# Layer 0's feed-forward: input projection by seven products of quarters

## The chip, the cores and the metric

One core of a Trainium2 chip. The metric is the time of one execution in device microseconds, median of the runs; lower is better.

## The reference

The kernel computes two transformer layers on one latent sequence of 256 tokens and one context of 256 tokens, with model width 1024. What the change touches is the gated feed-forward of layer 0, which both sequences pass (512 tokens together):

```python
def swiglu(h, w_in, w_out):
    a, u = jnp.split(h @ w_in, 2, axis=-1)
    return (jax.nn.silu(a) * u) @ w_out
...
D_FF = -(-(8 * D_MODEL) // (3 * 256)) * 256      # 2816
...
x_lat = x_lat + g2 * swiglu(rms_norm(x_lat, norm2_g[i]) * (1 + sc2) + sh2, ffn_w_in[i], ffn_w_out[i])
x_ctx = x_ctx + cg2 * swiglu(rms_norm(x_ctx, norm2_g[i]) * (1 + csc2) + csh2, ffn_w_in[i], ffn_w_out[i])
```

`w_in` is 1024 x 5632 (gate and up side by side), `w_out` is 2816 x 1024, all float32.

## The kernel before

Everything lies with features on the 128 partitions and tokens along the free axis: eight tiles of 128 features by 512 tokens, latent tokens in columns 0 to 255 (`LAT`), context tokens in 256 to 511 (`CTX`).

Every float32 product is made of three. A value is split into a high part (a copy to the `fp32r` type, on ScalarE, L402) and a low part (the value less its high part, on VectorE, L403). `prod` (L410) adds high x high, high x low and low x high into one PSUM bank. The activations' parts are `hh[k]` and `hl[k]`, made by `modulate` (L363 to L367) after each norm. A block of weights is loaded by a DMA on SyncE's queue into `w_raw` (two buffers), and split by `weights` into `w_hi` and `w_lo` (two buffers each).

`ffn(0, ...)` walks the inner width of 2816 (22 tiles of 128) in two chunks of 12 and 10 tiles. In a chunk, for each pair of tiles, it loads a gate block and an up block (1024 rows by 256 columns each), makes four banks of 512 tokens by 24 products each, and from them Silu(gate) x up, split again into `mid_h` and `mid_l` (L692 to L697). The first pair is made in two halves of 256 tokens, since the context's activations come later. Then four groups of 256 output columns (`mc`) multiply the chunk's mids by `w_out`, and VectorE adds the result, times a gate, onto the residual `x` (L446). After the last chunk the next norm's sums are taken from `x` (`after`).

Beside that run the ada steps (`ada_aside`): six parameter vectors of modulation, eight steps each. A step loads 128 rows of `ada_w` and multiplies and adds them onto one or two accumulators of 1024 columns on VectorE (L317, L319), two for the first three parameters (24 steps), one for the last three. `next(steps)` in the loops says where a step is written; here three per pair and two per `mc`.

The Tile framework orders each engine's instructions when the kernel is built, by priority and data dependence, and places all the semaphores. On the chip each engine runs its queue in that order. PSUM has eight banks of 512 float32 columns: `mixed()` hands out seven in turn, one is for ada.

GpSimd has next to no work in this stage. In the earlier attention layer it scales a bias table (L538) and masks it with two selects per half (L541, L545).

Of the kernel before, what the change touches and what calls it, by code (L numbers as in the profile page):

```python
# [8 lines left out]
F32 = mybir.dt.float32  # L9
F32R = mybir.dt.float32r  # L10
I32 = mybir.dt.int32
U8 = mybir.dt.uint8
AF = mybir.ActivationFunctionType
ALU = mybir.AluOpType
AX = mybir.AxisListType

P = 128
T = 512
D = 1024
KT = D // P  # L20
DFF = 2816
# [7 lines left out]
LAT = slice(0, 256)  # L29
CTX = slice(256, 512)  # L30
HALVES = ((0, LAT), (1, CTX))

NA_ADA = ((2,), (4,), (), (3,))
FFN_ADA = ((0, 5), (1, 1), (1, 0), (1, 2), (1, 4), (1, 3))


def cap(ap, off, dims):

    return bass.AP(ap.tensor, ap.offset + off, [list(ap.ap[0])] + [list(d) for d in dims])


class Block:
# [701 lines left out]
        ctx.close()  # L744


    def hgrn(self):
        nc = self.nc
        self.masks()
        yctx, ctx = ExitStack(), ExitStack()  # L750
# [6 lines left out]
        wi = self.in_hg_w_in[0]  # L757
        for hp in range(4):
            def wblock(i):
                return self.weights(wi[:, i * D + hp * 256 : i * D + (hp + 1) * 256])  # L760

            f = [[None, None], [None, None]]
            for d in range(2):
                w = wblock(3 + d)
                banks = [self.mm() for _ in range(2)]
# [8 lines left out]
            def project(i):  # L774
                w = wblock(i)
                if i == 1:
                    v = gp.tile([P, 4, 256], F32, name="hv", tag="hv")
                    for b in range(2):
                        ps = self.mm()
                        for j in range(2):  # L780
                            self.toks(ps[:, j * 256 : (j + 1) * 256], w, 2 * b + j)
                        nc.scalar.copy(v[:, 2 * b : 2 * b + 2].rearrange("p i c -> p (i c)"), ps)
                    return v
                ps = self.mm()
                for m in range(2):
                    self.feat(ps[:, m * 256 : (m + 1) * 256], w, m, LAT)
                t = gp.tile([P, T], F32, name=f"qg{i}", tag=f"qg{i}")
                nc.scalar.activation(t, ps, AF.Sigmoid)
                nc.vector.tensor_tensor(t, t, ps, op=ALU.mult)
                return t  # L790

            q = project(0)
# [6 lines left out]
            for m in range(2):  # L799
                h, on = 2 * hp + m, outs[m]  # L800
# [11 lines left out]
        wo = self.in_hg_w_o[0]  # L812
        self.norm_begin()
        for mc in range(4):
# [3 lines left out]
            else:  # L818
                own = lp if mc == 3 else None
                wh, wl = [[t[:, k] for k in range(KT)] for t in self.weights(block, pool=own)]  # L820
            one = self.mm()
            banks = [one[:, 0:256], one[:, 256:512] if mc < 3 else self.mm()[:, 0:256]]
# [178 lines left out]
    def finish(self, ctx):  # L1001
        nc = self.nc
        op = self.pool(ctx, "outp", 2)
        self.osb = [op.tile([P, 2, T], F32, name="osb", tag="osb") for _ in range(2)]

        def after(mt, s, c):
            half, q = mt // 4, mt % 4
            tp = self.mixed()
            for i in range(2):
                nc.tensor.transpose(tp[:, i * P : (i + 1) * P], self.x[mt][:, i * P : (i + 1) * P], self.ident)  # L1010
            nc.scalar.copy(
                self.osb[half][:, :, q * P : (q + 1) * P], tp[:, 0:256].rearrange("p (i c) -> p i c", i=2)
            )

            q0 = {3: 0, 5: 0, 6: 2, 7: 3}.get(mt)
            if q0 is not None:
                nc.sync.dma_start(
                    self.out[0, :, half * T + q0 * P : (mt + 1) * P].rearrange("(i p) c -> p i c", i=2),
                    self.osb[half][:, :, q0 * P : (q + 1) * P],
                )  # L1020

        return after

    def run(self):
        nc = self.nc
        self.setup()
        self.na_and_ada()

    def na_and_ada(self):
        self.na()  # L1030
        def after(mt, s, c):
            if mt == 0 and s == 0:
                self.norm_begin()
            self.norm_add(mt, c)
            if mt == KT - 1:
                self.norm_end(1, 0, s, c)

        self.ffn(0, slice(0, T), (12, 10), 14, after, lambda pool: self.ada_aside(FFN_ADA, pool))
        self.hgrn()
        with ExitStack() as ctx:  # L1040
            self.ffn(1, LAT, (NFF,), NFF, self.finish(ctx))
# [39 lines left out]
```

## Time and profile before

| what | value |
|---|---|
| runs | median 1169.7 us of 3 (1169.43 to 1171.44) |
| the profiled execution | 1168.13 us, its span 1166.3 us |
| TensorE busy | 1138.9 us, 98% of the span |
| VectorE busy | 778.7 us, 67% |
| ScalarE busy | 501.7 us, 43% |
| GpSimd busy | 74.5 us, 6% |

PE is TensorE, PEld its weight loads, DVE VectorE, ACT ScalarE, POOL GpSimd, SP SyncE. Matmuls are pipelined: one starts before the one in front has ended, so the time that a matmul costs is the distance between starts, not its duration. The same holds, by less, for neighbouring instructions on VectorE. In rows, a name such as `w_lo<-w_raw,w_hi` is output and inputs, `mm` and `ax` are PSUM banks, "L403" is the kernel's line, and "xN" says how many instructions a row holds.

### The profile page before, as it was taken

The numbers are of one execution on the slowest core, as the hardware profiler recorded it, in microseconds if no ns is written. First come the engines' busy times: TensorE is split into PE (matmuls) and PEld (weight loads), VectorE is DVE, ScalarE is ACT, GpSimd is POOL, SyncE is SP. The second block draws the span as 40 slices with busy tenths as digits, with TensorE's granted clock in tenths as the row PEclk, the third lists the DMA queues.
The fourth block names the chain that finished last, engine by engine and source line by source line (L and its number), as shares of the span: only waits on it lengthen the run. The fifth ranks groups of instructions, "written<-read, shape, count | busy, mean of one in ns | idle before, by whom it ended". The sixth has DMA issues, their size and how long they took to land.

```text
span 1166.3 us, 21342 instructions
## 1 busy us (share of the span) xinstructions
PE 1138.9 (98%) x8539; PEld 987.2 (85%) x8539; DVE 778.7 (67%) x1872; ACT 501.7 (43%) x1079; POOL 74.5 (6%) x121
## 2 busy tenths in 40 slices
PE   6979989999999999999999999999999999999998
PEld 5968869887898787878887889889797988999998
DVE  4579776966697664845353778686768687556553
ACT  5356564745462232213223344434243465545442
POOL 1045331410000000000000000000000000000000
PEclk9999999999999999999999999999999999999999
DMA  9785452433337442636352651323232345564562
GB/s 330 252 211 94 118 131 73 64 130 124 107 93 229 135 170 94 230 136 216 130 194 68 199 167 46 100 74 110 73 110 74 99 175 197 182 210 158 197 217 87
DMA packets 134403, 169.23 MB, mean 145 GB/s; under 512 B 4609, under 2 KB 122273, under 8 KB 134305
## 3 DMA queue, kind: packets, MB, share of 16 engines
q1 hardware_dynamic: 132368, 164.64, 42.5%
q0 software_dynamic: 1728, 3.17, 3.2%
q8 instruction: 67, 1.10, 0.4%
q14 instruction: 32, 0.25, 0.1%
q10 hardware_dynamic: 208, 0.07, 0.0%
HBM read 166.82 MB, written 1.05 MB: 144 GB/s over the span
## 4 chain that ended last, share of the span: by engine, by line
PE 90%; DVE 4%; DMA 3%; ACT 2%; issue 1%; ACTq 0%; DVEq 0%
PE mm L410 49%; PE ax L410 28%; DMA ada_raw<-in_ada_w_dram 3%; PE ada_ps L216 2%; PE ax L651 2%; PE ax L902 1%; PE ax L613 1%; PE ax L579 1%; PE ax L637 1%; PE ax L885 1%; PE ax L580 1%; PE ada_ps L266 1%; ACT qs L569 1%; DVE w_lo L403 1%; PE ax L948 1%; PE ax L659 1%
## 5 line engine op out<-in xcount | busy, mean ns | idle before, releaser
L403 DVE TENSOR_TENSOR w_lo<-w_raw,w_hi 128x512 fp32r<-128x512 f32 (+1 forms) x448 | 272.5, 644 | 128.4 <-ACT w_hi L402 126.0
L402 ACT CAST w_hi<-w_raw 128x512 fp32r<-128x512 f32 (+1 forms) x448 | 238.0, 583 | 230.6 <-PE mm L410 100.3
L410 PE MATMUL mm<-hl,w_hi 128*128 128x256 f32 (+1 forms) x608 | 201.6, 333 | 0.0
L410 PE MATMUL mm<-hh,w_lo 128*128 128x256 f32 (+1 forms) x608 | 201.3, 332 | 0.0
L410 PE MATMUL mm<-hh,w_hi 128*128 128x256 f32 (+1 forms) x608 | 199.1, 329 | 0.0
L410 PE MATMUL ax<-hh,w_lo 128*128 128x256 f32 (+1 forms) x400 | 131.7, 330 | 0.0
L410 PE MATMUL ax<-hh,w_hi 128*128 128x256 f32 (+1 forms) x400 | 131.7, 329 | 0.0
L410 PE MATMUL ax<-hl,w_hi 128*128 128x256 f32 (+1 forms) x400 | 131.3, 328 | 0.0
L410 PE MATMUL mm<-w_hi,hh 128*128 128x256 f32 x448 | 126.3, 282 | 0.8 <-ACT hh L366 0.8
L410 PE MATMUL mm<-w_lo,hh 128*128 128x256 f32 x448 | 125.7, 280 | 0.0
L410 PE MATMUL mm<-w_hi,hl 128*128 128x256 f32 x448 | 125.5, 280 | 0.0
L410 PEld LDWEIGHTS mm<-hl,w_hi 128*128 128x128 f32 x608 | 114.1, 188 | 11.4
L410 PEld LDWEIGHTS mm<-hh,w_lo 128*128 128x128 f32 x608 | 114.0, 188 | 11.3
L410 PEld LDWEIGHTS mm<-hh,w_hi 128*128 128x128 f32 x608 | 113.8, 188 | 10.9 <-ACT hh L366 0.8
L319 DVE SCALAR_TENSOR_TENSOR ada_acc<-ada_raw,cs,ada_acc 128x1024 f32<-128x1024 f32 x63 | 79.0, 1280 | 19.4 <-DMA ada_raw<-in_ada_w_dram 19.2
L410 PEld LDWEIGHTS mm<-w_hi,hh 128*128 128x128 f32 x448 | 84.6, 189 | 5.1 <-issue 3.2
L410 PEld LDWEIGHTS mm<-w_hi,hl 128*128 128x128 f32 x448 | 84.2, 188 | 2.0 <-issue 1.6
L410 PEld LDWEIGHTS mm<-w_lo,hh 128*128 128x128 f32 x448 | 84.2, 188 | 1.8 <-issue 1.4
L410 PEld LDWEIGHTS ax<-hh,w_hi 128*128 128x128 f32 x400 | 75.2, 188 | 7.6 <-ACT w_hi L402 0.8
L410 PEld LDWEIGHTS ax<-hl,w_hi 128*128 128x128 f32 x400 | 75.1, 188 | 7.4
L410 PEld LDWEIGHTS ax<-hh,w_lo 128*128 128x128 f32 x400 | 74.9, 187 | 7.4 <-DVE w_lo L403 0.2
L696 ACT CAST mid_h<-sa 128x512 fp32r<-128x512 f32 (+1 forms) x44 | 22.5, 512 | 92.8 <-DVE sa L693 92.8
(278 smaller groups left out, 2133.3 us busy)
## 6 DMA issues: line engine op xcount, KB each, us to landing
w_raw<-in_ffn_w_in_dram SPq DMA_DIRECT2D x44, 1024.0 KB, 5.1
ada_raw<-in_ada_w_dram SPq DMA_DIRECT2D x80, 512.0 KB, 4.6
w_raw<-in_hg_w_in_dram SPq DMA_DIRECT2D x20, 1024.0 KB, 4.8
w_raw<-in_na_w_qkv_dram SPq DMA_DIRECT2D x9, 1024.0 KB, 5.0
ada_first<-in_ada_w_dram SPq DMA_DIRECT2D x32, 256.0 KB, 5.9
w_raw<-in_ffn_w_out_dram SPq DMA_DIRECT2D x8, 896.0 KB, 4.5
w_raw<-in_ffn_w_out_dram SPq DMA_DIRECT2D x8, 768.0 KB, 4.3
w_raw<-in_ffn_w_out_dram SPq DMA_DIRECT2D x8, 640.0 KB, 4.3
```

Source lines behind the costliest of these rows:

```text
L216: nc.tensor.matmul(ps[32 * j : 32 * j + 32, 0:256], cs[:, k, :], w[:, j * 256 : (j + 1) * 256], start=(k == 0), stop=(k == last), tile_pos ...
L266: nc.tensor.matmul(ps[32 * j : 32 * j + 32, 0:P], self.cs[:, k, :], w[:, j // 2, (j % 2) * P : (j % 2 + 1) * P], start=(k == 0), stop=(k = ...
L319: eng.scalar_tensor_tensor(acc[s], w, c, acc[s], op0=ALU.mult, op1=ALU.add)
L402: self.nc.scalar.copy(wh[:, ks], raw[:, ks])
L403: self.nc.vector.tensor_tensor(wl[:, ks], raw[:, ks], wh.bitcast(F32)[:, ks], op=ALU.subtract)
L410: self.nc.tensor.matmul(out, a, b, start=(start and i == 0 and j == 0), stop=(stop and i == n - 1 and j == 2), skip_group_check=True,)
L569: nc.scalar.activation(cap(qa[half], P - 1, back), src, AF.Copy, scale=self.q_gain[own])
L579: nc.tensor.matmul(ps, qs[a][:, t], ks[a][:, kr], start=True, stop=False, skip_group_check=True)
L580: nc.tensor.matmul(ps, self.ql[a][:, t], ks[a][:, kr], start=False, stop=True, skip_group_check=True)
L613: nc.tensor.transpose(tp[:, kt * P : (kt + 1) * P], sb[:, kt * P : (kt + 1) * P], self.ident)
L651: nc.tensor.matmul(o[64 * a : 64 * a + 64, 0:256], v[:, kt, j * P + 64 * a : j * P + 64 * a + 64], pts[a][0][:, kt], start=(kt == 0), stop ...
L696: nc.scalar.copy(mh, sa)
```

## The change

The input projection of layer 0 goes to a new function, `ffn_seven`, which replaces `ffn(0, ...)`; the inner width is cut into chunks of 8, 8 and 6 tiles instead of 12 and 10. The first pair of tiles is still made plainly (`plain`). For every other block of 1024 x 256 weights, a `unit` cuts the weights into four quarters of 512 x 128 and the activations into four of 512 features x 256 tokens, and makes the block's product from seven products of quarters instead of eight (Strassen's method in Winograd's form). The sums of activations (`s1`, `s2`, `s3`, `s4`) are made once (`sums`); `s3` overwrites the context half of the activations. The differences of weights (`t13`, `t2`, `t4`) are made for each unit on GpSimd. Each product is four tiles deep, three products each, 256 columns wide: 12 matmuls, 84 in a unit. The two PSUM halves `x` and `z` of one bank and a part `y` of another collect them, and copies and adds on ScalarE and VectorE join them to the two output tiles.

The weights' parts lie in a ring of eight places of 4 x 128 columns (`quarter`) which units and output projection fill in turn. Units interlace: a unit's last two products are written between the products of the next. The matmuls' order within a chunk is fixed by `add_manual_dep`. The low parts of the mids, and half of the low parts of the output weights, move from VectorE to GpSimd. The ada steps are spread anew: three after the plain pair, then one per unit, one per two units, one per unit in the three chunks, and two to four per `mc`.

```diff
+    def quarter(self, src, eng=None):
+        nc, n = self.nc, src.shape[1]
+        s = self.place % 8
+        self.place += 1
+        hi, lo = [...]
+        nc.scalar.copy(hi, src)
+        (eng or nc.vector).tensor_tensor(lo, src, hi.bitcast(F32), op=ALU.subtract)
+        return hi, lo
+
+    def ffn_seven(self, chunks, after, aside):
...
+        def finish(g, mh, ml):
+            nc.scalar.copy(mh, g)
+            nc.gpsimd.tensor_tensor(ml, g, mh.bitcast(F32), op=ALU.subtract)
+
+        def plain():
+            quarters = []
+            raws = [w_in(0, up) for up in range(2)]
...
+            banks = [self.mixed() for _ in range(4)]
+            for s, r in HALVES:
+                for bank, q in zip(banks, quarters):
+                    self.prod(bank[:, r], ...)
+                for k in range(KT):
+                    (nc.gpsimd if s == 0 else nc.vector).tensor_tensor(
+                        f[s][k // 2][:, k % 2], self.hh[k].bitcast(F32)[:, r], self.hl[k].bitcast(F32)[:, r], op=ALU.add
+                    )
+            sums()
...
+        def sums():
+            a, c = f
+            for p in range(2):
+                for out, x, y, op in (
+                    (c[2 + p], c[p], c[2 + p], ALU.add),
+                    (c[p], a[p], c[p], ALU.subtract),
+                    (a[p], c[2 + p], a[p], ALU.subtract),
+                    (a[2 + p], a[2 + p], a[p], ALU.subtract),
+                ):
+                    nc.vector.tensor_tensor(out, x, y, op=op)
+            for p in range(2):
+                for src, (hi, lo), k in ((c[2 + p], s1s, 0), (a[p], s24, 0), (a[2 + p], s24, 4)):
+                    ks = slice(k + 2 * p, k + 2 * p + 2)
+                    nc.scalar.copy(hi[:, ks], src)
+                    nc.vector.tensor_tensor(lo[:, ks], src, hi.bitcast(F32)[:, ks], op=ALU.subtract)
+            for k in range(4):
+                src, hi, lo = c[k // 2][:, k % 2], self.hh[k], self.hl[k]
+                nc.scalar.copy(hi[:, CTX], src)
+                nc.vector.tensor_tensor(lo[:, CTX], src, hi.bitcast(F32)[:, CTX], op=ALU.subtract)
...
+        def unit(raw, up, g, mids):
...
+            xz, y = self.mixed(), self.mixed()[:, 0:256]
+            x, z = xz[:, 0:256], xz[:, 256:512]
...
+            t13 = fp.tile([P, 2, 4, P], F32, name="t13", tag="t13", bufs=1)
+            t2 = fp.tile([P, 4, P], F32, name="t2", tag="t2", bufs=1)
+            t4 = fp.tile([P, 4, P], F32, name="t4", tag="t4", bufs=1)
+            run(x, self.quarter(b11), a11, True)
+            nc.scalar.copy(u[0][:, LAT], x)
+            run(y, self.quarter(b21), a12, True)
+            nc.vector.tensor_tensor(u[0][:, LAT], u[0][:, LAT], y, op=ALU.add)
+            yield
+            nc.gpsimd.tensor_tensor(t13, ..., op=ALU.subtract)
+            nc.gpsimd.tensor_tensor(t2, b22, t13[:, 0], op=ALU.subtract)
+            run(z, self.quarter(t13[:, 0]), s1)
+            nc.scalar.copy(u[1][:, CTX], z)
+            run(x, self.quarter(t2), s2)
+            nc.scalar.copy(u[1][:, LAT], x)
+            yield
+            nc.gpsimd.tensor_tensor(t4, b21, t2, op=ALU.subtract)
+            run(z, self.quarter(b22), s4)
+            nc.vector.tensor_tensor(u[1][:, LAT], u[1][:, LAT], z, op=ALU.add)
+            yield
+            run(x, self.quarter(t13[:, 1]), s3)
+            nc.vector.tensor_tensor(u[1][:, CTX], x, u[1][:, CTX], op=ALU.add)
+            if up:
+                nc.vector.tensor_tensor(g[0][:, LAT], g[0][:, LAT], u[0][:, LAT], op=ALU.mult)
+                nc.vector.tensor_tensor(g[1], g[1], u[1], op=ALU.mult)
+                finish(g[1], *mids[1])
+            else:
+                nc.scalar.activation(g[0][:, LAT], g[0][:, LAT], AF.Silu)
+                nc.scalar.activation(g[1], g[1], AF.Silu)
+            yield
+            run(x, self.quarter(t4), a22)
+            if up:
+                nc.vector.tensor_tensor(g[0][:, CTX], g[0][:, CTX], x, op=ALU.mult)
+                finish(g[0], *mids[0])
+            else:
+                nc.scalar.activation(g[0][:, CTX], x, AF.Silu)
...
+        for si, nff in enumerate(chunks):
+            mid, chain, prev = [], [], None
+            if si == 0:
+                mid += plain()
+                more(3)
+            for fc in range(f0 + len(mid), f0 + nff, 2):
+                mids, g = [mid_tiles() for _ in range(2)], gates()
+                for up in range(2):
+                    this = unit(w_in(fc, up), up, g, mids)
+                    next(this)
+                    if prev:
+                        next(prev)
+                    next(this)
+                    if prev:
+                        next(prev, None)
+                    next(this)
+                    prev = this
+                    more((1, up, 1)[si])
+                mid += [tuple(m) for m in mids]
+            next(prev)
+            next(prev, None)
...
+                    for m in range(2):
+                        cuts = [0, nff // 2, nff]
+                        quarters = [
+                            (a, self.quarter(raw[:, a:b, m * P : (m + 1) * P], nc.gpsimd if a > 0 else nc.vector))
+                            for a, b in zip(cuts[:-1], cuts[1:])
+                        ]
+                        part_of(m, quarters, slice(0, T))
...
+                more(((2, 2, 2, 2), (2, 3, 3, 3), (4, 4, 2, 2))[si][mc])
...
-        self.ffn(0, slice(0, T), (12, 10), 14, after, lambda pool: self.ada_aside(FFN_ADA, pool))
+        self.ffn_seven((8, 8, 6), after, lambda pool: self.ada_aside(FFN_ADA, pool))
```

`run` issues for each of the four tiles the three matmuls of `prod`; only the first product into `x` and into `y` starts a new sum in its bank.

## Rows read from the trace of the kernel before

**Rows 1.** The page: busy time, TensorE's granted clock by slice, one DMA issue.

```profile
PE 1138.9 (98%) x8539; PEld 987.2 (85%) x8539; DVE 778.7 (67%) x1872; ACT 501.7 (43%) x1079; POOL 74.5 (6%) x121
...
PEclk9999999999999999999999999999999999999999
...
w_raw<-in_ffn_w_in_dram SPq DMA_DIRECT2D x44, 1024.0 KB, 5.1
```

**Rows 2.** The chain that ended last: start us, us, what.

```profile
342.07 5.65 PE ax L410 x48
347.73 5.51 PE mm L410 x24
...
404.14 10.99 PE mm L410 x48
```

**Rows 3.** Busy time by stretch of layer 0's feed-forward: us, PE, PEld, DVE, ACT, POOL.

```profile
325.00:349.00 24.00, 24.00 (x196) 23.55 (x196) 23.01 (x48) 13.81 (x30) 0.00 (x0) 1.00 0.35 104
349.00:460.00 111.00, 111.00 (x509) 89.72 (x507) 68.53 (x91) 32.52 (x61) 0.00 (x0) 1.00 0.49 160
460.00:512.00 52.00, 52.00 (x239) 41.32 (x236) 35.86 (x57) 11.30 (x27) 0.00 (x0) 1.00 0.55 178
512.00:642.00 130.00, 130.00 (x580) 105.27 (x580) 63.09 (x94) 36.59 (x69) 0.51 (x3) 1.00 0.46 153
642.00:692.00 50.00, 50.00 (x249) 41.87 (x248) 36.17 (x71) 20.08 (x49) 0.00 (x0) 1.00 0.62 199
```

**Rows 4.** Groups by line and shape from 300 us on: busy us, mean ns.

```profile
L403 DVE TENSOR_TENSOR w_lo<-w_raw,w_hi 128x512 fp32r<-128x512 f32 x315 | 204.3, 686 | 95.3 <-ACT w_hi L402 93.2
L402 ACT CAST w_hi<-w_raw 128x512 fp32r<-128x512 f32 x314 | 179.8, 619 | 128.9 <-PE ax L410 46.5 <-PE mm L410 44.8 <-issue 27.6
...
L410 PE MATMUL mm<-hh,w_hi 128*128 128x256 f32 x352 | 97.9, 281 | 0.0
...
L693 DVE TENSOR_TENSOR sa<-sa,ax 128x256 f32<-128x256 f32 x12 | 5.0, 419 | 14.5 <-PE ax L410 14.5
...
L692 ACT ACTIVATE sa<-ax 128x256 f32<-128x256 f32 x12 | 4.6, 381 | 2.3 <-PE ax L410 2.3
```

**Rows 5.** VectorE's instructions in order of time, merged: start us, us, what.

```profile
327.25 0.75 DVE L403 TENSOR_TENSOR w_lo<-w_raw,w_hi 128x256 fp32r<-128x256 f32 x2
...
337.94 0.87 DVE L367 SCALAR_TENSOR_TENSOR hl<-ht,mod,hh 128x256 fp32r<-128x256 f32 x2
...
339.39 2.47 DVE L319 SCALAR_TENSOR_TENSOR ada_acc<-ada_raw,cs,ada_acc 128x1024 f32<-128x1024 f32 x2
...
346.54 2.50 DVE L403 TENSOR_TENSOR w_lo<-w_raw,w_hi 128x512 fp32r<-128x512 f32 x4
```

**Rows 6.** The chain at a hand-over from TensorE to ScalarE.

```profile
318.67 0.02 issue
318.69 0.48 ACT rs_y L352
```

**Rows 7.** GpSimd and VectorE in order of time, at two places in attention.

```profile
121.72 1.16 POOL L541 TENSOR_SCALAR_AFFINE_SELECT tb<-tb 64x576 f32<-64x576 f32 x1
122.94 1.56 POOL L545 TENSOR_SCALAR_AFFINE_SELECT tb<-tb 64x576 f32<-64x576 f32 x2
...
122.98 0.71 DVE L441 SCALAR_TENSOR_TENSOR rq_y<-rq_b,rq_y 128x8 f32<-128x8 f32 x1
...
123.93 0.59 DVE L440 SCALAR_TENSOR_TENSOR rq_b<-rq_b,qk_ss 128x8 f32<-128x8 f32 x1
...
75.36 2.14 POOL L538 TENSOR_SCALAR tb<-tb 128x768 f32<-128x768 f32 x1 [7.56 <-DMA tb<-in_na_rpb_dram]
...
75.47 0.73 DVE L441 SCALAR_TENSOR_TENSOR rq_y<-rq_b,rq_y 128x8 f32<-128x8 f32 x1
...
76.24 0.17 DVE L439 TENSOR_TENSOR rq_b<-rq_y 128x8 f32<-128x8 f32 x1
```

**Rows 8.** One line's instructions on GpSimd: duration ns, least, median, most.

```profile
L545 POOL TENSOR_SCALAR_AFFINE_SELECT tb<-tb x16: 735/741/1150, 79.8 to 236.8; 64x576 f32<-64x576 f32 x16
```

More of the change, by code (lines that the diff above doesn't have):

```diff
@@ L744, in ffn @@
         ctx.close()
+    def quarter(self, src, eng=None):
+        nc, n = self.nc, src.shape[1]
+        s = self.place % 8
+        self.place += 1
+        hi, lo = [
+            t[s // 4].rearrange("p k c -> p (k c)")[:, s % 4 * 512 : s % 4 * 512 + n * P].rearrange(
+                "p (k c) -> p k c", c=P
+            )
+            for t in self.ring
+        ]
+        nc.scalar.copy(hi, src)
+        (eng or nc.vector).tensor_tensor(lo, src, hi.bitcast(F32), op=ALU.subtract)
+        return hi, lo
```

107 lines of the change are left out of this document (added).

## The prediction

> **What bounds the kernel now.** [...] Busy matmuls overlap, so the second view is the chain that ended last. In layer 0's feed-forward (about 323 to 692 us of the span) it is PE with hardly a gap, so the rate of matmuls is the price. Forty-eight products of 512 columns take 10.99 us, 229 ns each; forty-eight of 256 columns take 5.65 us, 117.7 ns each, although each loads weights of its own [rows 2]. Halving the width thus costs almost nothing per column, and removed columns are removed time, as long as PE stays the bound. So the third view is the other engines by stretch: VectorE (DVE) is busy 23.0 of 24.0 us in the first 24 us of this stage, then 68.5 of 111, 35.9 of 52, 63.1 of 130 and 36.2 of 50; GpSimd (POOL) does next to nothing there [rows 3]. The fourth view, groups and neighbouring instructions, gives prices: a low part of 512 columns lasts 686 ns, but four in a row take 2.50 us, so one more costs 0.60; two accumulations of 1024 take 2.47, one more costs 1.19; at 256 columns one more costs 0.34 (two in 0.75) to 0.40 (two in 0.87) [rows 4, 5]. The chain before the stage ends the first pair of column tiles at 347.73 [rows 2].
>
> **Part 1, fewer columns.** A weight block (1024 by 256) took 2 x 8 x 3 = 48 products of 512 columns: 10.99 us. A unit of seven takes 7 x 4 x 3 = 84 of 256: 84 x 0.1177 = 9.89. Twenty of the 22 blocks become units (the first pair stays plain, in halves of 256 columns as before): 20 x 1.10 = **-22.0 us** if PE sets the pace everywhere.
>
> **Part 2, a wait inside each unit.** x and z are halves of one PSUM bank. The order written for PE puts t13[0] into z and right behind it t2 into x, and ScalarE (ACT) must copy z in between. The trace shows no write to one half of a bank beside a read of the other, so whether PE waits is open: bounds 0 and a full round trip. That is the matmul's end 0.28, the hand-over 0.02, a 256-column read by ACT 0.38, the hand-over 0.02, less the pitch of 0.12 = 0.58 us [rows 4, 6]. I take 0.58, as the program's tile holds both halves: PE's pace is 10.47 per unit, 20 x 0.58 = 11.6 of the 22.0 given back. [...] Queued behind a waiting PE is its whole order, since it is fixed by hand. The other reuses of a bank have at least one product group of 12 x 0.118 = 1.41 us between them, which hides the same round trip.
>
> **Part 3, work for DVE and POOL, per unit.** The seven parts need seven low parts of 512 columns on DVE: 7 x 0.60 = 4.2 us (before: four). Added on DVE are three adds from PSUM, 3 x 0.34 = 1.0; the gate products (512, 256 and, from PSUM, 256 columns) are 1.28 per pair of units, 0.64 per unit, of which 0.47 read two operands from SBUF. The ada steps, two accumulations of 1.19 each up to step 24 and one afterwards, fall one per unit in chunk 0 (2.4 us), one in two units with two accumulations in chunk 1 (1.2), one per unit with one in chunk 2 (1.2). DVE alone: 8.2 us in chunk 0, 7.0 later, below PE's 10.47. ACT: 7 x 0.62 for the high parts [rows 4], 2.5 for three copies of 0.38, Silu and the mids: 6.8, hidden. DMA: one block of 1024 KB landing in 5.1 us per unit, hidden [rows 1].
>
> POOL gets t13 (1024 columns), t2, t4 and half a pair's mid parts (512 each): 2560 columns, two inputs. The trace has no such operation on POOL. What it has are readers of one input: a select of 576 columns, 0.74 us undisturbed, and a scaling of 768 columns [rows 7, 8]. And it shows what they do to DVE: a DVE instruction on eight columns with two SBUF inputs, usually 0.17 us, lasted 0.71 beside a select that had begun 0.04 earlier, and the next caught 0.59, each to that select's end; beside the scaling it lasted 0.73, and was free again 0.84 after the scaling began [rows 7]. So while POOL reads, DVE operations with two SBUF inputs stand still; a select is stretched to 1.16 where DVE was first [rows 7]. Such operations are the low parts, the gate products and the ada accumulations. [...]
>
> POOL's hold per unit: 576 inputs hold 0.74 and 768 hold 0.84; a line through these two gives 0.97 for 1024 inputs and 1.50 for 2048, so 3 x 0.97 + 1.50 = 4.4 us; in proportion to the select (1.29 ns an input) it is 6.6. Below both lies one pass over both inputs at once, 3.3. I take the middle of 4.4 and 6.6, **5.5**. Port time per unit: 5.5 + 4.2 + 0.47 + ada = 12.6 us in chunk 0 and 11.4 in chunks 1 and 2, against 10.99 before.
>
> Chunk 0, six units: 6 x 1.6 = **+9.6**. Chunks 1 and 2, fourteen units: at 11.4 they would be +0.4 each, +5.6. But while the output projection of the chunk before runs, DVE has time, and the ring of eight holds a unit's seven parts in advance: 4.2 of DVE and 60% of POOL's 5.5, 7.5 us per chunk, 15 for both, against an excess over PE's pace of 14 x 0.9 = 13. With all of this lead PE paces them: 14 x -0.52 = -7.3. I take the middle, **-0.8**.
>
> **Part 4, the sums of activations.** DVE is full until the last low activation at about 338.8 [rows 5]. Then come 8 adds of 256 (2.7), 8 of 512 (4.8), six low parts of 512 and four of 256 (5.0), two products (1.2) and unit 0's first three low parts (1.8): 15.5 us, to 354.3. PE would be through the plain pair at 347.7 and through the two groups that need no sum at 350.5, so the third waits at least 3.8. POOL's eight adds of 256 (0.7 each) can hold DVE for 5.6 more, 9.4; three ada steps ahead in the queue (6.1) make 15.5. I take **+7**.
>
> **Part 5, chunk ends.** Units interlace; the first of a chunk has no partner for one more adjacent wait (0.58), the last none for two (0.62 each): 1.8 x 3 = 5.5, of which chunk 0, paced by DVE, hides its share: **+3.6**, bounds 0 and 5.5.
>
> **Costed at nothing.** The output projection keeps its 528 products of 512 columns. A third pass adds 16 residuals of 0.40 on DVE, 6.4 us, hidden by PE's 11.0 (8.2 in chunk 2) per column group; there the subtractions moved to POOL relieve DVE. In chunk 2's first two groups DVE and POOL have 10 us of work for PE's 8.2: if the ada steps stand ahead of a low part that is +4. Uncovered, all this is +10.
>
> Sum: 9.6 - 0.8 + 7 + 3.6 = +19.4. The profiled execution took 1168.1 us (span 1166.3); 1187.5 on that basis. The median of the runs is 1.6 higher: **1189**.
>
> **The rivals.** (A) The forecast: DVE and POOL share a port and set the pace. With the hold at 4.4 chunk 0 gives +3, the rest -7.3, the start 3.8, the ends 3.6: 1173. At 6.6: 16 + 21 + 9.4 + 5.5 = +52: 1222. (B) The port costs little, the bank waits remain: 20 x -0.52 = -10.4, +5.5, +3.8: 1169. For it: POOL's readers sometimes ran beside DVE without loss. (C) The other side: two halves of a bank don't wait for each other and POOL holds at most 3.3 per unit, so port time is 9.2 to 10.4 and PE keeps 117.7 ns: -22.0 + 3.8: **1151.5**. It decides from the point where a unit's other work, POOL's hold included, is below 9.9. For it: rows 2 and DVE's slack in rows 3; against it: the two long eight-column rows. (D) Everything on DVE, the reads from PSUM too, stands still while POOL works, at 6.6: 14.8 and 13.6 per unit, 6 x 3.8 + 14 x 2.6 = 59, start 15.5, ends 5.5: +80, 1250. Against it: only two-input operations were seen held.
>
> **Chances.** A 0.48, B 0.14, C 0.28, D 0.10. The measurement tells 0.2% (2.3 us) from no change. Faster: C, 0.05 of B and 0.01 of A, 0.34. Same: 0.05 of B, 0.01 of A, 0.06. Slower: the rest, 0.60. A alone spans 1173 to 1222; to leave no more than 2 in 10 out, the range reaches down through C, to 1148, and leaves out D and C's lower edge.
>
> **What would show it.** Right: two-input POOL operations of 512 columns near 1.2 us; DVE low parts well above 0.69 us beside them; PE's longest waits are for low parts, and 0.6 us gaps before t2's group; a gap of several us near 350; unit pitch near 12.6, then 11. Wrong: unit pitch 9.9 with no gaps (C), 10.5 with only the bank gap (B), or POOL operations under 0.7 us. The weakest terms are POOL's price, which no row has, and the lead of the ring.

## The result and the profile after

The changed kernel takes 1277.3 us (median of four runs, 1271.5 to 1280.3) beside 1170.6 for the kernel before (four runs): ratio 1.0905, 95% interval 1.0864 to 1.0946. The prediction was 1189 in a range of 1148 to 1222: the direction was right, the size was not (107 us instead of 19). The profiled execution took 1271.53 us, its span 1269.7, which is 103.4 us more than the span before.

The page of the changed kernel, to be read against [rows 1]:

```profile
PE 1154.9 (91%) x9235; PEld 1027.3 (81%) x9235; DVE 915.4 (72%) x1975; ACT 564.9 (44%) x1194; POOL 264.3 (21%) x233
...
PEclk9999999999979889899999889999999999999999
```

PE's busy share fell from 98% to 91%, and the granted clock, flat before, dips in the stage's slices. GpSimd's busy time rose by 190 us, VectorE's by 137.

PE's instructions in order of time, at the seams of the stage (start us, us, what, in brackets the wait ahead of it):

```profile
345.71 0.58 PE L410 MATMUL mm<-hl,w_hi 128*128 128x256 f32 x1 [4.30 <-DVE hl L367]
358.55 0.28 PE L867 MATMUL mm<-hh,w_hi 128*128 128x256 f32 x1
...
367.00 0.58 PE L867 MATMUL mm<-hh,w_lo 128*128 128x256 f32 x1 [8.05 <-DVE w_lo L759]
...
512.23 0.39 PE L867 MATMUL ax<-hh,w_hi 128*128 128x256 f32 x1
...
683.67 0.36 PE L867 MATMUL ax<-hh,w_hi 128*128 128x256 f32 x1
...
797.72 0.59 PE L348 MATMUL ax<-acc,ones 128*128 128x256 f32 x2
```

The plain pair ends at 358.55 (347.73 in [rows 2]) and the first unit stands until 367.00. From there the seams give each chunk with its output projection: 145.2, 171.4 and 114.1 us. At the old prices (10.99 a block, 120.9 in all for the output, 5.5 per tile of inner width) they would be 109.9, 131.9 and 98.9, which is an estimate. So the start cost 10.8 + 8.5 = 19 us, chunk 0 35, chunk 1 40, chunk 2 15: 109 in sum, of which 103 is left at the end of the span. With the output projection at its old price, a unit took about 16.9 us in chunk 0, 15.9 in chunk 1 and 13.5 in chunk 2.

PE's waits from 323 to 812 us (what waited, for whom: us in total, times, longest):

```profile
PE ax L867 <- ACT u L897: 13.6, 6, 4.3
PE ax L867 <- ACT g L897: 13.4, 4, 4.8
PE mm L867 <- ACT g L897: 10.3, 5, 3.6
PE mm L867 <- DVE w_lo L759: 8.1, 1, 8.1
...
PE ax L867 <- DVE u L903: 5.5, 4, 2.3
PE mm L410 <- DVE hl L367: 4.5, 2, 4.3
```

All waits of this view add up to 87 us; in the kernel before, the same view of this stage is empty. L897 is ScalarE's copy of z, for which the wait of Part 2 stands; 37.3 us are in the three rows shown. With its fourth row, the copies of x (L899) and the additions of z (L903), some 59 us lie at the reuse of the one bank, 2.9 per unit. For GpSimd's own results PE waits directly in three places, 7.5 us in all, for low parts of the mids (L790).

Busy time of the units' stretches (us, PE, PEld, DVE, ACT, POOL, granted clock, DMA share, GB/s), to be read against [rows 3]:

```profile
358.00:461.00 103.00, 73.54 (x532) 68.24 (x530) 97.37 (x106) 39.28 (x80) 46.59 (x24) 0.90 0.42 134
513.00:638.00 125.00, 95.70 (x712) 89.99 (x712) 116.05 (x125) 49.74 (x100) 58.57 (x32) 0.92 0.50 164
684.00:770.00 86.00, 72.36 (x541) 68.74 (x539) 56.62 (x83) 37.83 (x77) 38.65 (x24) 0.92 0.31 102
```

VectorE is nearly full in chunks 0 and 1 (95% and 93%), not in chunk 2 (66%), where PE is slow all the same. The groups from 323 to 812 us say what fills it (busy us, mean ns):

```profile
L891 POOL TENSOR_TENSOR t<-w_raw 128x1024 f32<-128x1024 f32 x20 | 52.2, 2608 | 130.8 <-DVE w_lo L759 102.1 <-DVE gs L244 22.9 <-DMA w_raw<-in_ffn_w_in_dram 5.8
...
L319 DVE SCALAR_TENSOR_TENSOR ada_acc<-ada_raw,cs,ada_acc 128x1024 f32<-128x1024 f32 x63 | 108.9, 1740 | 4.6 <-DMA ada_raw<-in_ada_w_dram 4.6
L759 DVE TENSOR_TENSOR w_lo<-t,w_hi 128x512 fp32r<-128x512 f32 x80 | 69.0, 872 | 18.7 <-ACT w_hi L758 17.2
L759 DVE TENSOR_TENSOR w_lo<-w_raw,w_hi 128x512 fp32r<-128x512 f32 x80 | 68.1, 859 | 34.0 <-ACT w_hi L758 33.7
...
L909 DVE TENSOR_TENSOR g<-g,u 128x512 f32<-128x512 f32 x10 | 15.2, 1518 | 0.2
```

A low part lasts 872 or 859 ns (686 in [rows 4]), the wide gate product 1518 where a 512-column operation with nothing beside it takes 690, an ada accumulation 1740 (1280 before, the mean of its 63): 63 x 0.46 + 80 x 0.19 + 80 x 0.17 + 10 x 0.83 = 66 us. I take them as VectorE's time held, and the version below that gives all of GpSimd's work to VectorE bears it out: there the same operations are back at 686, 685 and 1280 ns. And GpSimd itself stood 102 us before its t13 until the one buffer of the old t13 had been read.

Two places in order of time over all engines, one ahead of the plain pair's context half and one wait of chunk 0:

```profile
339.84 3.01 DVE L363 SCALAR_TENSOR_TENSOR ht<-x,gs,rs_y 128x256 f32<-128x256 f32 x2
340.09 2.48 POOL L891 TENSOR_TENSOR t<-w_raw 128x1024 f32<-128x1024 f32 x1 [5.77 <-DMA w_raw<-in_ffn_w_in_dram]
...
432.49 2.44 POOL L891 TENSOR_TENSOR t<-w_raw 128x1024 f32<-128x1024 f32 x1 [5.59 <-DVE w_lo L759]
...
433.00 2.48 DVE L909 TENSOR_TENSOR g<-g,u 128x512 f32<-128x512 f32 x1
...
434.97 0.62 ACT L758 CAST w_hi<-t 128x512 fp32r<-128x512 f32 x1 [2.89 <-POOL t L891]
...
435.52 0.62 ACT L789 CAST mid_h<-g 128x512 fp32r<-128x512 f32 x1
...
436.04 0.37 ACT L897 COPY g<-ax 128x256 f32<-128x256 f32 x1
436.46 0.39 PE L867 MATMUL ax<-s24h,w_hi 128*128 128x256 f32 x1 [2.02 <-ACT g L897]
...
437.35 0.42 PE L867 MATMUL ax<-s24h,w_hi 128*128 128x256 f32 x1
437.56 0.42 PE L867 MATMUL ax<-s24l,w_hi 128*128 128x256 f32 x1
...
440.80 0.28 PE L867 MATMUL ax<-hh,w_lo 128*128 128x256 f32 x1
440.91 0.28 PE L867 MATMUL ax<-s24h,w_hi 128*128 128x256 f32 x1
```

In the first, unit 0's t13 runs as soon as its weights have landed, amid the context's norm, and two steps of the norm on VectorE last 3.01 us (0.87 without it). In the second, z's products are over, but its copy (0.37 us, 436.04) stands in ScalarE's queue behind a cast that waits for GpSimd's t13 and behind a cast of a mid that waits for the gate product, which t13 holds (2.48 us instead of 0.69). PE resumes 0.05 us after the copy. Soon after, matmuls start 0.21 us apart until about 440.6 (the granted clock is 0.51 from 437.3 to 440.6); then 0.12 again, at a clock of 1.00. The mean granted clock of this execution is 0.972, so such stretches cost, by estimate, at most 0.028 x 1269.7 = 36 us. Some of them lie in the waits and would be counted twice: over the trace, 30 of the 36 us fall on time in which PE is busy. So -22 of columns, +87 of waits and +30 of clock make +95 of the 103 measured; the other 8 are not attributed.

### The profile page after: what moved, and what is told of

It reads as the page before. It is cut to its first block, busy times and chain, and to the rows that moved or that the text cites. A ratio compares the mean times of both kernels' runs of the same rounds, so it can differ in the third digit from the quotient of the medians.

```text
span 1269.7 us, 23302 instructions
## 1 busy us (share of the span) xinstructions
PE 1154.9 (91%) x9235; PEld 1027.3 (81%) x9235; DVE 915.4 (72%) x1975; ACT 564.9 (44%) x1194; POOL 264.3 (21%) x233
## 5 line engine op out<-in xcount | busy, mean ns | idle before, releaser
L410 PE MATMUL mm<-hl,w_hi 128*128 128x256 f32 (+1 forms) x456 | 144.1, 319 | 4.7 <-DVE hl L367 4.5
L410 PE MATMUL mm<-hh,w_lo 128*128 128x256 f32 (+1 forms) x456 | 142.1, 314 | 0.0
L410 PE MATMUL mm<-hh,w_hi 128*128 128x256 f32 (+1 forms) x456 | 141.0, 314 | 0.8 <-ACT hh L366 0.8
L319 DVE SCALAR_TENSOR_TENSOR ada_acc<-ada_raw,cs,ada_acc 128x1024 f32<-128x1024 f32 x63 | 108.9, 1740 | 4.6 <-DMA ada_raw<-in_ada_w_dram 4.6
L410 PEld LDWEIGHTS mm<-hh,w_hi 128*128 128x128 f32 x456 | 86.1, 190 | 6.6 <-ACT hh L366 2.0
L758 ACT CAST w_hi<-t 128x512 fp32r<-128x512 f32 x80 | 49.1, 619 | 85.5 <-POOL t L891 37.0
L759 DVE TENSOR_TENSOR w_lo<-t,w_hi 128x512 fp32r<-128x512 f32 x80 | 69.0, 872 | 18.7 <-ACT w_hi L758 17.2
L891 POOL TENSOR_TENSOR t<-w_raw 128x1024 f32<-128x1024 f32 x20 | 52.2, 2608 | 130.8 <-DVE w_lo L759 102.1
L410 PE MATMUL ax<-hh,w_hi 128*128 128x256 f32 x232 | 64.2, 277 | 0.5 <-ACT w_hi L402 0.5
L410 PE MATMUL ax<-hh,w_lo 128*128 128x256 f32 x232 | 64.2, 277 | 0.2 <-DVE w_lo L403 0.2
```

Source lines behind the costliest of these rows:

```text
L319: eng.scalar_tensor_tensor(acc[s], w, c, acc[s], op0=ALU.mult, op1=ALU.add)
L410: self.nc.tensor.matmul(out, a, b, start=(start and i == 0 and j == 0), stop=(stop and i == n - 1 and j == 2), skip_group_check=True,)
L758: nc.scalar.copy(hi, src)
L759: (eng or nc.vector).tensor_tensor(lo, src, hi.bitcast(F32), op=ALU.subtract)
L891: nc.gpsimd.tensor_tensor(t13, cap(raw, P, [[4 * 256, 2], [256, 4], [1, P]]), cap(raw, 0, [[P, 2], [256, 4], [1, P]]), op=ALU.subtract,)
```

## The experiments

The theory after the result: GpSimd's operations hold VectorE, which then paces chunks 0 and 1 and starves PE; the wait for the shared bank, long because the copy stands in ScalarE's queue, is second. The rival: the shared bank is the main thing, and GpSimd matters little. Unless a count is given, a run below is one execution. Executions of the kernel before beside them took 1164 to 1178 us and those of the changed kernel 1272 to 1280, so differences of less than some 10 us between two single executions say little.

**z in a bank of its own.**

```diff
-            x, z = xz[:, 0:256], xz[:, 256:512]
+            x, z = xz[:, 0:256], self.mixed()[:, 0:256]
...
-            run(z, self.quarter(t13[:, 0]), s1)
+            run(z, self.quarter(t13[:, 0]), s1, True)
```

> z gets a PSUM bank of its own, so that no group of products writes into a bank that ScalarE or VectorE still has to read for the group before. Theory Q (the wait is in the queues): TensorE's order, fixed by hand, stops at bank reuse, and the reader stands in ScalarE's queue behind casts whose source GpSimd has not made; the 59 us of TensorE waits for L897, L899 and L903 go, and with them part of the clock loss: 1185 to 1215 us. Theory P (the port): VectorE and GpSimd, which hold each other, set the pace, the bank wait is only the place where TensorE happens to stand; its waits move to the low parts and the time stays above 1255.

1250.9: 26 us back, far from the level of before and in neither range, just below that of theory P. Part of the waits moves to VectorE's additions of x (L906, three rows of 6.7, 5.8 and 3.2 us), and 11 us of L897 stay.

**The other unit's product between z and x**: a `yield` behind the copy of z, and the loop calls `next(this)` twice before `next(prev)`.

> x and z still share a bank, but TensorE's order puts the other unit's product between z from t13[0] and x from t2, so that every reuse of a bank has a group of 1.41 us in between. Theory Q: the longest wait (L897, 38.5 us) shrinks by 1.4 us in each of 20 units, and some clock comes back: 1230 to 1250 us. Theory P: unchanged, 1265 to 1280.

1252.2: nearly the same by other means, 2 us above the range of theory Q.

**GpSimd's work on VectorE**: every `nc.gpsimd.tensor_tensor` of `ffn_seven` becomes `nc.vector.tensor_tensor`.

> All work of the changed stage that was on GpSimd goes to VectorE. Theory P: nothing holds anything, VectorE has 10 us per unit (11.2 in the first chunk), about TensorE's 10.5: 1180 to 1200 us. Theory Q: the differences come sooner, but the copies out of PSUM still stand behind casts in ScalarE's queue: 1200 to 1240 us. If GpSimd's help were worth its hold, it would be slower than with it: above 1277.

1198.1, 79 us back, although VectorE now has all the work; it is at the upper end of theory P's range. The rival falls.

**Both.**

> All on VectorE and z in a bank of its own. In the run with all on VectorE, TensorE waits 14.5 us for L897 and L899 and 13.5 for low parts. If bank reuse is a cost of its own, those 14.5 and a little clock go: 1178 to 1188 us. If the waits only move to the low parts: 1193 to 1200.

1178.8. The four runs make a square: 1277 and 1251 with GpSimd, 1198 and 1179 without. GpSimd costs 79 or 72 us, the shared bank 26 or 19. A full VectorE alone is not the loss: from 358 to 461 us it is busy 100.6 of 103 us in this run, and PE is busy 92.9 of them instead of 73.5. What counts is how much of the busy time is hold. PE at the seams of chunk 1 here:

```profile
480.14 0.39 PE L867 MATMUL ax<-hh,w_hi 128*128 128x256 f32 x1
...
558.20 0.39 PE L410 MATMUL ax<-mid_h,w_hi 128*128 128x512 f32 x1
...
559.59 0.33 PE L867 MATMUL ax<-hh,w_hi 128*128 128x256 f32 x1
...
561.05 0.39 PE L410 MATMUL ax<-mid_h,w_hi 128*128 128x512 f32 x1
```

Eight units in 80.9 us less 1.4 of output projection: 9.94 each, Part 1's 9.89. What is left is at the start:

```profile
PE mm L867 <- DVE w_lo L759: 12.1, 2, 11.8
PE ax L867 <- DVE w_lo L759: 3.2, 4, 1.7
```

**The hold by itself**, a kernel with only these operations:

> Not the reference's computation: only the disputed operations, one stretch after the other. VectorE subtractions of 512 columns alone (6), GpSimd subtractions of 512 alone (6), GpSimd differences of 1024 strided columns as t13 (4), then 8 of GpSimd beside 16 of VectorE with both inputs in SBUF, 8 beside 16 of VectorE with one input in PSUM, 8 beside 16 casts of ScalarE. If the two engines exclude each other for whole instructions, the first mixed stretch lasts the sum (8 x 1.1 + 16 x 0.6 = 18 us) and the second the longer of both (about 9.6); if not, both last about 9.6. GpSimd alone: 1.0 to 1.3 us for 512 columns, 1.5 to 2.6 for 1024.

Engines in order of time (start us, us, what):

```profile
6.83 4.32 DVE L1069 TENSOR_TENSOR dvo<-key,xt 128x512 f32<-128x512 f32 x6
...
11.88 7.96 POOL L1069 TENSOR_TENSOR poo<-key,xt 128x512 f32<-128x512 f32 x6 [11.43 <-ACT key L1075]
...
21.29 9.59 POOL L1091 TENSOR_TENSOR big<-wr 128x1024 f32<-128x1024 f32 x4 [1.45 <-DVE wr L1089]
...
31.57 19.11 DVE L1069 TENSOR_TENSOR dvo<-key,xt 128x512 f32<-128x512 f32 x16 [10.35 <-ACT key L1075]
31.61 13.44 POOL L1069 TENSOR_TENSOR poo<-key,xt 128x512 f32<-128x512 f32 x8 [0.73 <-ACT key L1075]
...
51.51 11.52 DVE L1069 TENSOR_TENSOR dvo<-key,ps 128x512 f32<-128x512 f32 x16
51.55 10.70 POOL L1069 TENSOR_TENSOR poo<-key,xt 128x512 f32<-128x512 f32 x8 [6.50 <-DVE key L1077]
...
63.86 10.36 ACT L1109 COPY aco<-key 128x512 f32<-128x512 f32 x16 [32.33 <-DVE key L1077]
63.90 10.68 POOL L1069 TENSOR_TENSOR poo<-key,xt 128x512 f32<-128x512 f32 x8 [1.65 <-DVE key L1077]
```

Sixteen VectorE operations take 11.52 us beside GpSimd when one input lies in PSUM (0.72 each, as alone) and 19.11 when both lie in SBUF: each GpSimd operation of 512 columns holds VectorE for 7.59 / 8 = 0.95 us. GpSimd's operation itself goes from 1.33 alone to 1.68. ScalarE is not held (16 copies in 10.36 us, 0.65 each where a single one lasts 0.62, and GpSimd's at 1.33 as alone). At these prices, holds of whole instructions would make 8 x 1.33 + 16 x 0.72 = 22.2 us of the first mixed stretch, so its 19.11 are less; the 18 of the expectation came near by its lower prices. The hold of 0.95 is more than the 0.72 that VectorE takes to do such a subtraction itself. Three of 512 per unit and one of twice that make 3 x 0.95 + 1.9 = 4.75 us, an estimate that lets the hold go with the columns: between the prediction's 4.4 and its 5.5. So in this run VectorE's operations with both inputs in SBUF are held, by 0.95 us and not by all of the 1.68 that the GpSimd operation lasts, and those with one input in PSUM by 0.

**The hold without its results, and the results without it.** Differences left out, quarters read in their place, and all other work on VectorE; then GpSimd makes the differences and nobody reads them; then they are read:

```diff
-            nc.gpsimd.tensor_tensor(t13, ...); nc.gpsimd.tensor_tensor(t2, ...); nc.gpsimd.tensor_tensor(t4, ...)
-            run(z, self.quarter(t13[:, 0]), s1)
+            run(z, self.quarter(b12), s1)
...
```

> Leaves out the differences of weights: the quarters themselves go in their places, so the product is another one; all that GpSimd still did in the changed stage goes to VectorE. This is the unit with neither hold nor a chain through a difference. VectorE has 7.0 to 8.2 us per unit, below TensorE's 10.5, so only the bank waits at their bare price (0.58 per unit) and the wait for the sums at the start (about 13 us) should be left: 1170 to 1182 us.

> As the run that leaves the differences out, but GpSimd makes all of them, in full size and from the same weights, and nobody reads them. Only the hold is added. If the hold alone costs VectorE its time: 4.3 us more per unit (2.15 for 1024 columns, 1.08 for each 512), 11.3 to 12.5 against TensorE's 10.5: 1190 to 1215 us. If only the chain through the differences costs: the same as without them, within 4 us.

> GpSimd makes the differences and they are read; the low parts of the mids and of the output weights go to VectorE. Against the run with unread differences this adds the chain from a difference through ScalarE's cast and VectorE's low part to TensorE, and what stands in the two queues behind it. If the hold is the whole cause: as the run with unread differences, within 6 us. If the chain in the queues counts as well: 15 to 40 us above it.

1206.8, 1262.6 and 1255.5. GpSimd's differences, which nobody waits for in the second, cost 56 us; waiting for them adds nothing (-7). Two expectations missed: the first run was not faster than the run without GpSimd (the next one shows why), and the second is far above 1215. VectorE's low parts of weights in the first and in the second run, where they are stretched by 45 us in sum:

```profile
L759 DVE TENSOR_TENSOR w_lo<-w_raw,w_hi 128x512 fp32r<-128x512 f32 (+1 forms) x192 | 126.4, 678 | 42.3 <-ACT w_hi L758 41.6
```

```profile
L759 DVE TENSOR_TENSOR w_lo<-w_raw,w_hi 128x512 fp32r<-128x512 f32 (+1 forms) x192 | 171.7, 915 | 44.2 <-ACT w_hi L758 43.8
```

A rival of the hold is that GpSimd, which reads the loaded weights, keeps their buffer and so delays the next transfer. In the second run SyncE's queue waits 167 us for VectorE's low parts before it loads a block, and never for GpSimd, so there the transfers are late because VectorE is.

> Leaves out the differences of weights (the product is another one), nothing on GpSimd, and z in a bank of its own. The run without differences but with the shared bank took 1207 with 22 us of waits for L892 and L894. If those come from the bank together with ScalarE's queue, in which the copy stands behind casts that wait for a place in the ring, they go: 1165 to 1178 us. If the loss is elsewhere: above 1195.

1172.8, as expected, so 34 us of it were the shared bank.

**VectorE's time given back.** The ada accumulations of this stage shortened, with both banks, and in the kernel before:

```diff
-                        eng.scalar_tensor_tensor(acc[s], w, c, acc[s], op0=ALU.mult, op1=ALU.add)
+                        f = slice(0, 64 if (pool is not None and (l, m) in FFN_ADA) else D)
+                        eng.scalar_tensor_tensor(acc[s][:, f], w[:, f], c, acc[s][:, f], op0=ALU.mult, op1=ALU.add)
```

> The changed kernel, GpSimd and the shared bank as they are; the ada steps beside layer 0's feed-forward accumulate only the first 64 of 1024 columns, the rest of their sums is left out. That takes about 1.6 us from each of 63 accumulations on VectorE, some 2 per unit in chunk 0 and 1 per unit in chunk 1. If the holds cost time because VectorE is then full (97.4 of 103 us in chunk 0, 116.1 of 125 in chunk 1), the stage gives back about 6 x 3.2 + 8 x 1.6 = 32 us, 1240 to 1250. If they cost time because PE waits for copies that stand behind GpSimd's differences, less than 10: above 1262.

> The same ada steps cut to 64 columns (the rest of their sums is left out), with z in a bank of its own. The run with z's own bank alone took 1251. If VectorE's time is what is left, 32 us less, 1215 to 1225; if the chain through GpSimd is, above 1240.

> The kernel before with the same cut of the ada steps (the rest of their sums is left out): VectorE has slack there, so no change beyond 0.5% by either theory, 1165 to 1175; it is the control for the two runs beside it.

1241.3, 1204.1 and 1166.0 (before beside them 1171.7; the last is within the spread that runs of it have). The first hit its range, the second came out 11 us below its own. So 36 us come back with the shared bank, 47 with z in a bank of its own, against 79 and 72 that GpSimd costs. The cut takes more than held time off VectorE, since the accumulations' own work goes too, so how large the share of a full VectorE is stays open. In the first of these, chunk 0:

```profile
358.00:461.00 103.00, 80.88 (x584) 75.02 (x583) 76.27 (x122) 44.65 (x89) 46.05 (x28) 0.93 0.49 164
```

VectorE has slack now (76 of 103), and PE still waits: over the stage 42 us in four rows for the copy of z.

**The lead.** Two buffers for t13, for which one buffer of the mids makes room; the control has the mids alone:

> The changed kernel with eight buffers for the mids instead of nine, which frees the room that the next run needs; it is that run's control. Eight is what a chunk uses, so only the first mids of chunks 1 and 2 can come to wait for the last output group of the chunk before: 1277 with up to 5 more.

> The same with two buffers for t13. In the changed kernel GpSimd stood 102 us before its t13 differences until the low part of the old t13 had been read, so a unit's parts can't be made a unit ahead, whatever the ring holds. If this lack of lead is what breaks the prediction's step on the ring, the difference goes out early, the copies of z no longer stand behind it, and the time falls by 20 us or more against the control. If VectorE's time (full in chunks 0 and 1) is what counts, it falls by less than 10.

1275.3 and 1262.8: 12 us, between both expectations and little more than single executions differ by. GpSimd's idle time before t13 for a low part falls from 100.4 to 23.3 us, and most of the loss stays.

**A hold where VectorE has slack**, and three chunks, each in the kernel before (`(nc.gpsimd if l == 0 else nc.vector)` for the mids' low parts; chunks `(8, 8, 6)`):

> The kernel before with only the low parts of layer 0's mids on GpSimd, 22 subtractions of 512 columns. GpSimd holds VectorE 1.1 us once in 16 us there, and VectorE has slack. By the theory that the hold costs only where VectorE has none: ratio 0.998 to 1.002. If any hold costs its length, 22 x 1.1 = 24 us: 1.02.

> The kernel before with chunks of 8, 8 and 6 and 12 places for the mids. A third pass of 16 residuals on VectorE is hidden: ratio 0.998 to 1.003. If the chunks were a cost of their own, a boundary would show a gap of TensorE and the ratio would be above 1.005.

1170.6, ratio 0.999 (0.9968 to 1.0012), and 1173.9, ratio 1.0036 (1.002 to 1.0052). The hold costs nothing there, although VectorE was held: an ada accumulation lasted 1361 ns instead of 1280 and a low part of weights 736 instead of 686, some 11 us in sum. Three chunks cost 4 us, a little more than expected.

**Towards a better version.** No GpSimd, own bank, and two plain pairs ahead of the units, so that the sums have more cover:

> All on VectorE, z in a bank of its own, and two plain pairs ahead of the units instead of one, so that VectorE has a second pair's 22 us for the sums of activations before a unit needs them (two units fewer, 18). If the 11.8 us wait of TensorE at the start is the sums, it goes for 1.5 us of lost units: 1166 to 1172 us, at or below the kernel before. If VectorE is as far behind anyway, 1176 to 1182.

1171.4 (ten runs), ratio 1.0016 (0.9995 to 1.0036): level. Its largest wait of the stage:

```profile
PE mm L410 <- DVE w_lo L759: 9.7, 1, 9.7
```

It is at the second plain pair, whose low parts stand behind the sums in VectorE's queue. So the sums were made behind that pair:

```diff
-            (sums if fc == 0 else sums_of_context)()
+            if fc:
+                sums()
+                sums_of_context()
```

> As the run with two plain pairs, no GpSimd and z in a bank of its own, but all sums of activations are made after the second plain pair's products are written, so that VectorE comes to that pair's eight low parts before the sums; one ada step moves. There PE stood 9.7 us at the second pair (349 to 361) and then ran 11 us at a granted clock of 0.76. If that wait is all that keeps the seven products from showing their gain, the time is 9.7 + 2.6 below that run: 1158 to 1160, a ratio to the kernel before of 0.990. If VectorE, which is busy 65.6 of 68 us right after, is only late elsewhere instead, the wait moves to the first units and the time stays within 0.2% of the kernel before, 1168 to 1173.

1166.1 (five runs) beside 1171.7, ratio 0.9951 (0.9937 to 0.9965): 0.5% faster than the kernel before, half of what was expected. The windows behind that place in the two versions, first with the sums in front, then late (columns as above):

```profile
349.00:361.00 12.00, 2.65 (x23) 2.44 (x21) 12.00 (x19) 4.54 (x9) 0.00 (x0) 0.79 0.13 40
361.00:372.00 11.00, 10.61 (x71) 10.62 (x72) 10.96 (x14) 0.00 (x0) 0.00 (x0) 0.76 0.75 239
372.00:440.00 68.00, 67.35 (x525) 63.59 (x524) 65.56 (x102) 35.20 (x70) 0.00 (x0) 1.00 0.52 172
```

```profile
349.00:361.00 12.00, 12.00 (x104) 12.00 (x103) 12.00 (x21) 5.33 (x9) 0.00 (x0) 1.00 0.53 176
361.00:372.00 11.00, 11.00 (x96) 11.00 (x95) 10.75 (x13) 4.70 (x10) 0.00 (x0) 1.00 0.47 142
372.00:440.00 68.00, 62.50 (x432) 57.07 (x431) 63.58 (x98) 30.02 (x61) 0.00 (x0) 0.95 0.45 149
```

The big wait is gone; some 5.5 us of idle time and a clock of 0.95 appear in the first units (0.7 us and 1.00 with the sums in front), where VectorE is busy 63.6 of 68 us. Part of the wait moved, as the other expectation had it. These two traces show only where the waits lie: their executions took 1166.3 us with the sums in front, the fastest of ten, and 1167.75 with the sums late, the slowest of five, so the 5 us between the medians can't be read from them.

## Why the prediction was wrong

**Part 1 was right.** The columns' gain is there: 9.94 us per unit once nothing else is late, against the 9.89 of the sum, so -21.0 us instead of -22.0.

**Part 3 failed, in its use of the hold, not in its price.** GpSimd's hold was put at 5.5 us per unit, and the run of it alone gives 4.75. That the two engines share a port, as the forecast has it, no run shows: what the runs show is the hold of 0.95 us. But the step "the ring of eight holds a unit's seven parts in advance", which absorbed all of the excess in chunks 1 and 2 and left -0.8, does not hold: those chunks cost 40 + 15 us (the two thirds of Part 5 among them). Chunk 0 cost 35 instead of 9.6. The sum also let the slower of the two paces be a unit's whole time, 12.6 us where the prediction's port time sets it and 10.47 where PE does; the units took about 16.9, 15.9 and 13.5, more than either, so the delays did not hide each other. Three things stand in its place. VectorE is busy for 95% and 93% of the time in the units of chunks 0 and 1, and in the whole stage some 66 us of its time is hold; taking the ada work off it gives 36 to 47 us. Parts can't be made ahead, since t13 has one buffer and GpSimd waits 102 us for it; two buffers give 12. And late results pass through ScalarE's queue to PE, as the place at 436 us shows. That the hold is the main cause is shown (56 us with nobody reading the differences, 72 to 79 with all of GpSimd's work); how the loss divides between a full VectorE, the queues and the bank is not, since the effects overlap.

**Part 2 was right in its mechanism, and its term too small.** The wait for the bank is there, but at 59 / 20 = 2.9 us per unit instead of 0.58. The round trip was priced as if the copy stood alone; the trace shows it behind casts that wait for GpSimd, VectorE or a place in the ring. Without GpSimd the shared bank costs 19 us in one pair of runs and 34 in the pair without differences, 1.0 to 1.7 per unit and still above its price.

**Part 4 was too small:** 19 us instead of 7. The wait of 8.1 us alone is about what it took. But the plain pair, too, ended 10.8 us later, 4.3 of it in one wait for a low activation; behind that wait the granted clock was 0.50 from 346 to 350 us and 0.77 in the next four, some 3 us more, and 0.9 us the execution was late already ahead of the stage. The prediction did not have unit 0's differences there; GpSimd, with an empty queue, made them at 340 us, and their hold fell on the norm that this activation comes from. In the run without GpSimd the plain pair ends at 350.1 and the unit goes on at 362.3 instead of 367.0, although that execution came to the stage 1.4 us later, so some 6 of the 19 us are GpSimd's. Most of the others I put down to the sums: the wait for a low part behind them is 11.8 us in that run, and as long in the run without differences.

**Part 5 and the third pass.** The third pass, costed at nothing with up to +10, cost 4 us in the kernel before. Part 5, the chunk ends, was not measured by itself.

**A term was missing.** The granted clock, 1.00 in all of this stage before, fell in all unit stretches (0.90 to 0.92), which cost 30 to 36 us. The sum counted waits as their own length only.

**The rivals.** D, given 0.10 and 1250, was nearest in time, and its mechanism is refuted: operations that read PSUM were not held (0.72 us). A's mechanism, the hold, is the one that ruled, but its upper end of 1222 had neither the missing lead nor the queues nor the clock. B falls with the runs without GpSimd and C with the price of the hold, 4.75 against at most 3.3. Of the signs named ahead, PE's longest single wait was for a low part (8.1 us), but the largest sum was for the copies of z.

## What to carry to other kernels

Work moved to GpSimd need not relieve VectorE: here each subtraction of 512 columns held a VectorE that had two-input work in SBUF for 0.95 us, more than the 0.72 that VectorE takes for it. That was free where VectorE had slack (ratio 0.999 with the mids' low parts of the kernel before on GpSimd) and dear where VectorE feeds the engine that sets the pace (56 us for differences that nobody reads). A held instruction shows as busy, only longer (a low part 872 ns instead of 686), so compare its mean with that of the same instruction undisturbed. Price a wait with everything that stands ahead of the releasing instruction on its engine, and ask of each early-made buffer how many there are before counting on a lead. Waits of PE cost more than their length here: 87 us of them came with 30 us of lower clock, so new work belongs where PE's queue has cover. Without GpSimd, with a bank of its own for z and the sums behind a second plain pair, the loss of 9% became a gain of 0.5%.

## What the runs showed of the hardware

A GpSimd subtraction of 512 float32 columns takes 1.33 us alone and 1.68 beside VectorE operations of two SBUF inputs, and there holds VectorE for 0.95; VectorE operations with one input in PSUM stay at 0.72. A subtraction of 1024 columns with strided inputs takes 2.40 us alone and 2.61 in the mean in the changed kernel. Soon after a wait of 2.0 us PE's matmuls of 256 columns started 0.21 us apart until 440.6 us, at a granted clock of 0.51, and 0.12 apart behind that, at 1.00; in the version with two plain pairs, after a wait of 9.7 us, the mean granted clock was 0.76 over the next 11.
